# The decoded samples' state update, moved forward beside the branch projections, in a one-core hybrid decoder step

## The chip, the cores and the metric

The kernel runs on one core of one Trainium2 chip. The metric is the device time of one execution in microseconds. A core has TensorE (PE in the profile), VectorE (DVE), ScalarE (ACT), GpSimd (POOL) and SyncE (SP). Each works off its own queue in order; transfers are issued from the queues of SyncE, GpSimd and, seldom, ScalarE, and run on 16 DMA engines.

## The reference

One layer of a decoder trunk for 1024 prompt tokens and 8 decoded samples of one token each, 1024 channels wide, in float32. The part that matters here is the gated delta rule of the samples, with a state S of 128 x 128 for each of 8 samples (`b`) and 8 heads (`h`):

```python
def step(S, inp):
    q_t, k_t, v_t, b_t, g_t = inp
    S = S * jnp.exp(g_t)[..., None, None]
    delta = (v_t - jnp.einsum('bhk,bhkv->bhv', k_t, S)) * b_t[..., None]
    S = S + jnp.einsum('bhk,bhv->bhkv', k_t, delta)
    return S, jnp.einsum('bhk,bhkv->bhv', q_t, S)
...
y_a = _gdn_out(o_a, gdn_gate, lp['gdn_onorm_w']) @ lp['w_gdn_out']
...
y_b = o_b @ lp['w_swa_out']
mix = (jax.nn.sigmoid(ga) * y_a + jax.nn.sigmoid(gb) * y_b) @ lp['w_o']
```

The new states are an output, and the normed and gated result of the samples is the last eight columns of the input of `w_gdn_out`. `y_b` and `y_a` are the two branches.

## The kernel before

The 1032 tokens stand in the free dimension in three parts (`PARTS`): part 0 and part 1 of 384 tokens, part 2 of 264, the samples being its last 8. A projection (`project`) takes one block `j` of 128 output channels and one part `t`: 8 steps over the inner dimension with three matmuls each, because each operand is split into a high and a low half (`split`: ScalarE makes the high half at L129, VectorE the low one at L130). A weight block of 512 KB is loaded from SyncE's queue into a room `raw` (L135) and split into `wh` and `wl`. There is one room `raw` and two each of `wh` and `wl`.

`branches` does first the rest of the branch `w_swa_out` (14 projections: part 0 of six blocks, part 1 of all eight), and then the branch `w_gdn_out` with all three parts. Beside the 14 projections runs the generator `sample_delta`: before each projection one step of it is traced, up to its next `yield`. Its steps are: activation and squares of the samples' q, k, v; their norms (a matmul, `rows_rsqrt` with a power on GpSimd, `rows_spread` with a matmul); keys and queries `kq`; the products of k and q with the old states, 32 matmuls for each half of the heads (L1172); transposes (L1180); the deltas `dl`; their transpose and a store to a DRAM room `dlr` (L1194); the output's norm, which gives `osm`; and the new states.

For the new states of head `h` (L1210 to L1219), `dlr[h]` is read back, broadcast to all 128 partitions, into one of two rooms `d` in turn (L1214, SyncE). ScalarE multiplies it by the key, eight times, one for each sample (L1216); VectorE scales the old state and adds (L1217); GpSimd's queue stores the head's states (L1219). The rooms lie in `b1l`, the states in `b1h` and `b1l`, and the weights and parts of the next branch are loaded while this goes on.

The order on each engine is fixed when the kernel is built, by a planner that simulates the engines: an instruction goes to its queue when it is planned to be ready, and among those ready the one traced first. `issue_after(ins)` adds one rule: what is traced inside comes behind `ins` on the engine of `ins`. Here it puts the step's matmuls behind the last matmul of the projection before, and the step's transfers on SyncE behind the last weight load. It binds nothing on ScalarE, VectorE or GpSimd.

Of the kernel before, what the change touches and what calls it, by code (L numbers as in the profile page):

```python
# [12 lines left out]
AF = mybir.ActivationFunctionType  # L13
ALU = mybir.AluOpType
# [4 lines left out]
P = 128  # L19
NP = 1024  # L20
NS = 8
NT = NP + NS
KC = 8
H = 8
# [5 lines left out]
EARLY = (3, 4)  # L30
# [10 lines left out]
def bc(ap, dim, n):  # L41

    a = ap.unsqueeze(dim)
    shape = list(a.shape)
    shape[dim] = n
    return a.broadcast_to(shape)


def carver(*rooms):

    used = [0] * len(rooms)

    def small(*shape, r=0):
        n = 1
        for x in shape:
            n *= x
        v = rooms[r][:, used[r]:used[r] + n]
        used[r] += n
        letters = "abcd"[:len(shape)]
        return v.rearrange(f"p ({' '.join(letters)}) -> p {' '.join(letters)}", **dict(zip(letters, shape)))  # L60

    return small


class Step:
# [1055 lines left out]
    def sample_delta(self, pool2):  # L1121

        nc, I = self.nc, self.I
        zl, cw = self.zl, self.cw
        S0, load = self.S0, self.load_state
        small = carver(*(self.flat_room(pool2, "b2", x, 2) for x in "hl"))
        act, tmp = small(24, NS), small(24, NS)
        nc.vector.tensor_tensor(act, zl[:, 3:11, :].rearrange("p b c -> p c b"), bc(cw[:, 3, :], 2, NS), op=ALU.mult)
        nc.vector.tensor_tensor(act, act, self.gsp, op=ALU.add)
        nc.scalar.activation(tmp, act, AF.Tanh, scale=0.5)  # L1130
        nc.vector.scalar_tensor_tensor(act, tmp, 1.0, act, op0=ALU.add, op1=ALU.mult)

        flat = lambda a: a.rearrange("p a h b -> p (a h b)")
        f3 = lambda a: a.rearrange("p h b -> p (h b)")
        qk = act[:, 0:16, :].rearrange("p (a h) b -> p a h b", a=2)
        v = act[:, 16:24, :]
        sq = small(2, H, NS)
        nc.vector.tensor_tensor(sq, qk, qk, op=ALU.mult)
        wide = small(H, NS, 2 * NS)
        nc.gpsimd.memset(wide, 0.0)  # L1140
        yield
        c, db = (self.flat_room(self.b1, "b1", x, 2) for x in "hl")
        load(6, c)
        load(7, c)
        ps = self.t(self.psm, [P, 1], "mm")
        nc.tensor.matmul(ps, flat(sq), self.ones[:, 0:1], start=True, stop=True)
        r = self.rows_rsqrt(small, ps, P, 1.0, 4 * EPS)
        yield
        rl = self.rows_spread(*r).rearrange("p (a h b) -> p a h b", a=2, h=H)
        kq = self.const([P, H, NS, 2], "kq")  # L1150
        nc.vector.tensor_tensor(kq[:, :, :, 0], qk[:, 1], rl[:, 1], op=ALU.mult)
        nc.vector.scalar_tensor_tensor(kq[:, :, :, 1], qk[:, 0], P ** -0.5, rl[:, 0], op0=ALU.mult, op1=ALU.mult)
        for i in range(2):
            nc.vector.tensor_copy(wide.rearrange("p h b c -> p h (b c)")[:, :, i::2 * NS + 2], kq[:, :, :, i])
        yield
        pr = small(H, NS)
        nc.vector.tensor_tensor(pr, kq[:, :, :, 0], kq[:, :, :, 1], op=ALU.mult)
        dots = self.t(self.psm, [P, H, NS], "mm")
        nc.tensor.matmul(f3(dots), self.ones, f3(pr), start=True, stop=True)
        qkd = small(H, NS)  # L1160
        nc.vector.tensor_copy(qkd, dots)
        yield
        eg = self.egb[:, :, 0, :].rearrange("p b h -> p h b")
        beta = self.egb[:, :, 1, :].rearrange("p b h -> p h b")

        rows = small(2, P, r=1)
        nc.gpsimd.memset(rows, 0.0)
        for i in range(2):
            ps = self.t(self.psm, [P, P], "mm")
            for b in range(NS):  # L1170
                for h in range(4):
                    nc.tensor.matmul(ps[32 * h:32 * h + 2 * NS], wide[:, 4 * i + h, b, :], S0[4 * i + h][:, b, :],  # L1172
                                     start=b == 0, stop=b == NS - 1)
            for h in range(4):
                at = slice(32 * h, 32 * h + 2 * NS)
                (nc.scalar.copy if h % 2 else nc.vector.tensor_copy)(rows[at, i, :], ps[at])
            yield
        pks = self.t(self.psm, [P, 2 * P], "mm")
        for i in range(2):
            self.transpose(pks[:, i * P:(i + 1) * P], rows[:, i, :])  # L1180
        pks = pks.rearrange("p (h c) -> p h c", c=32)[:, :, :2 * NS].rearrange("p h (b a) -> p h b a", a=2)
        yield
        pk, dl, o = small(H, NS, 2), small(H, NS), small(H, NS)
        nc.vector.tensor_tensor(pk, pks, bc(eg, 3, 2), op=ALU.mult)
        nc.vector.tensor_scalar_mul(dl, v, 0.5)
        nc.vector.tensor_tensor(dl, dl, pk[:, :, :, 0], op=ALU.subtract)
        nc.vector.tensor_tensor(dl, dl, beta, op=ALU.mult)
        yield
        ps = self.t(self.psm, [H * NS, P], "mm")
        self.transpose(ps, f3(dl))  # L1190
        dlT = small(P, r=1)[:H * NS]
        nc.vector.tensor_copy(dlT, ps)
        dlr = self.t(self.dr, [H, NS, P], "dlr")
        nc.sync.dma_start(dlr.rearrange("h b v -> (h b) v"), dlT)  # L1194
        yield
        nc.vector.tensor_tensor(o, qkd, dl, op=ALU.mult)
        nc.vector.tensor_tensor(o, o, pk[:, :, :, 1], op=ALU.add)

        nc.vector.tensor_tensor(pr, o, o, op=ALU.mult)
        yield  # L1200
        ps = self.t(self.psm, [H * NS, 1], "mm")
        nc.tensor.matmul(ps, f3(pr), self.ones[:, 0:1], start=True, stop=True)
        r = self.rows_rsqrt(small, ps, H * NS, 1.0 / P, EPS)
        yield
        rl = self.rows_spread(*r).rearrange("p (h b) -> p h b", h=H)
        nc.vector.tensor_tensor(o, o, rl, op=ALU.mult)
        self.osm = self.const([P, H, NS], "osm")
        nc.vector.scalar_tensor_tensor(self.osm, o, self.onw, self.sgs, op0=ALU.mult, op1=ALU.mult)

        for h in range(H):  # L1210
            if h % 4 == 0:
                yield
            d = db[:, h % 2 * NP:h % 2 * NP + NP].rearrange("p (b v) -> p b v", b=NS)
            nc.sync.dma_start(d, dlr[h].unsqueeze(0).broadcast_to([P, NS, P]))  # L1214
            for b in range(NS):
                nc.scalar.activation(d[:, b, :], d[:, b, :], AF.Copy, scale=kq[:, h, b, 0:1])  # L1216
                nc.vector.scalar_tensor_tensor(S0[h][:, b, :], S0[h][:, b, :], self.egb[:, b, 0, h:h + 1], d[:, b, :],  # L1217
                                               op0=ALU.mult, op1=ALU.add)
            nc.gpsimd.dma_start(self.O[3][0][:, h].rearrange("b k v -> k b v"), S0[h])  # L1219

    def rows_rsqrt(self, small, ps, n, scale, eps):

# [109 lines left out]
    def branches(self, pool, pool2):  # L1332
        nc, I = self.nc, self.I
# [3 lines left out]
        samples, rows = self.sample_delta(pool2), self.last_rows()  # L1337
# [15 lines left out]
        weights = lambda j: self.load_w(I["w_swa_out"][0][:, j * P:(j + 1) * P])  # L1353
        ws = {j: weights(j) for j in (0, 1)}
        late = [(j, 0) for j in range(8) if j not in EARLY]
        for j, t in (*late[:2], *((j, t) for j in range(7) for t in (0, 1) if t or (j, t) in late[2:]), (7, 1), *late[-1:] * (7 not in EARLY)):
            with self.tc.issue_after(self.last_mm), self.tc.issue_after(self.w_load.ins):
                next(samples, None)
                if j > 3:
                    next(rows, None)  # L1360
            self.project(ws[j], ob, yb_out, (t,))
            if t and j < 6:
                ws[j + 2] = weights(j + 2)
            if t and j in (3, 4):
                with self.tc.issue_after(self.w_load.ins):
                    if j == 3:
                        oa = {0: self.load_part(pool2, self.oa, 0, rooms=first)}
                    else:
                        nc.sync.dma_start(ub[2], self.ubd[2].rearrange("j p n -> p j n"))
                        for j1 in EARLY:  # L1370
                            nc.sync.dma_start(ub[0][:, j1, :], self.ubd[0][j1])
# [700 lines left out]
```

## Time and profile before

| | |
|---|---|
| three runs | 2075.94, 2079.22 and 2079.28 us; median 2079.22 |
| the profiled execution | 2079.57 us, with a span of 2077.9 us from first to last instruction |
| mean granted clock of TensorE | 0.991 |
| DMA | 275.75 MB, mean 133 GB/s; 212.93 MB read from HBM |
| the branch `w_swa_out` beside the samples | about 1122 to 1188 us of the span |
| scalings of the states (L1216) | 1178.4 to 1218.3 us |
| stores of the states (L1219) | 1182.1 to 1220.5 us |

Times in rows are microseconds from the start of the span. A row of the timeline has start, duration, engine, line, operation, output and inputs, a count, and in brackets the idle time before it and what ended that. A row of the waits has who waited, for whom, the total, the number of waits and the longest. In rows by stretch the busy time and the number of instructions of each engine come first, then the granted clock, the DMA engines' busy share and GB/s.

### The profile page before, as it was taken

What the parts mean: (1) busy time and instruction counts of PE and PEld (TensorE: products, weight loads), DVE (VectorE), ACT (ScalarE), POOL (GpSimd) and SP (SyncE); (2) the same over time, 40 slices, a digit from 0 to 9 for tenths busy, and PEclk for the clock granted to TensorE, in tenths of its full rate; (3) what the DMA queues carried; (4) which work ended last, traced back from release to release, by engine and by line L of the source; (5) the groups of instructions that cost most, each with busy time, mean ns of one, the idle gap of its engine ahead of it and who ended that gap; (6) DMA issues with size and microseconds to landing.
All of it is one profiled execution on the core that took longest, in us unless ns stands there. A gap on an engine that the chain in (4) does not pass through costs nothing.

```text
span 2077.9 us, 41299 instructions
## 1 busy us (share of the span) xinstructions
PE 2011.2 (97%) x16245; PEld 1908.0 (92%) x16245; DVE 1353.8 (65%) x2714; ACT 900.6 (43%) x2233; POOL 521.6 (25%) x594
## 2 busy tenths in 40 slices
PE   7999999999999999989989999999999999999997
PEld 4987877799999999989989999999999999999997
DVE  4755767483655746656554575578886776778866
ACT  4664545443334343442442442345544544544443
POOL 2000000121321211211111000105566556443552
PEclk9999999999999999999999999999999999999999
DMA  8256443332322322312276874423233233487773
GB/s 292 72 145 206 138 168 116 94 99 66 82 82 57 77 70 52 91 41 57 67 200 186 257 225 133 144 65 97 88 106 113 88 97 92 135 294 271 268 261 114
DMA packets 301887, 275.75 MB, mean 133 GB/s; under 512 B 59730, under 2 KB 248111, under 8 KB 301676
## 3 DMA queue, kind: packets, MB, share of 16 engines
q1 hardware_dynamic: 295642, 252.14, 39.6%
q0 software_dynamic: 5552, 20.37, 2.8%
q8 instruction: 127, 2.08, 0.4%
q10 hardware_dynamic: 498, 0.61, 0.1%
q14 instruction: 68, 0.56, 0.1%
HBM read 212.93 MB, written 62.51 MB: 133 GB/s over the span
## 4 chain that ended last, share of the span: by engine, by line
PE 79%; DMA 8%; DVE 6%; ACT 3%; issue 2%; POOL 1%; SPq 1%; DVEq 0%; POOLq 0%; ACTq 0%
PE mm L180 18%; PE mm L181 18%; PE mm L182 18%; PE wv L180 2%; PE wv L182 2%; PE wv L181 2%; DMA ws<-in_w_ffn_down_dram 2%; PE pv L652 1%; PE wy L180 1%; PE wy L181 1%; PE wy L182 1%; DMA raw<-in_w_swa_out_dram 1%; PE pt L190 1%; PE tp L190 1%; PE mm L264 1%
## 5 line engine op out<-in xcount | busy, mean ns | idle before, releaser
L180 PE MATMUL mm<-b1h,wh 128*128 128x384 f32 (+1 forms) x1520 | 496.9, 328 | 4.2 <-ACT gt L1294 1.6
L181 PE MATMUL mm<-b1l,wh 128*128 128x384 f32 (+1 forms) x1520 | 489.4, 323 | 0.0
L182 PE MATMUL mm<-b1h,wl 128*128 128x384 f32 (+1 forms) x1520 | 487.7, 323 | 0.3 <-DVE wl L130 0.3
L180 PEld LDWEIGHTS mm<-b1h,wh 128*128 128x128 f32 x1520 | 286.5, 189 | 13.1 <-issue 4.6
L181 PEld LDWEIGHTS mm<-b1l,wh 128*128 128x128 f32 x1520 | 286.7, 189 | 5.1 <-issue 3.1
L182 PEld LDWEIGHTS mm<-b1h,wl 128*128 128x128 f32 x1520 | 286.0, 189 | 3.9 <-issue 2.8
L129 ACT ACTIVATE wh<-raw 128x1024 fp32r<-128x1024 f32 x83 | 87.0, 1049 | 124.3 <-PE mm L181 72.9
L130 DVE TENSOR_TENSOR wl<-raw,wh 128x1024 fp32r<-128x1024 f32 x82 | 101.3, 1236 | 59.9 <-ACT wh L129 57.4
L181 PE MATMUL mm<-pk,w 128*128 128x260 f32 (+1 forms) x440 | 124.6, 283 | 1.1 <-DVE pk L130 1.1
L180 PE MATMUL mm<-pk,w 128*128 128x260 f32 (+1 forms) x440 | 124.5, 283 | 0.0
L182 PE MATMUL mm<-pk,w 128*128 128x260 f32 (+1 forms) x440 | 124.4, 283 | 0.0
L130 DVE TENSOR_TENSOR w<-ws,w 128x512 fp32r<-128x512 f32 x88 | 77.8, 885 | 36.4 <-ACT w L129 36.2
L1626 ACT COPY bml<-mm 128x256 f32<-128x256 f32 (+1 forms) x132 | 48.9, 371 | 100.7 <-PE mm L182 98.9
L180 PE MATMUL mm<-bmh,w 128*128 128x260 f32 (+1 forms) x320 | 90.3, 282 | 0.0
L182 PE MATMUL mm<-bmh,w 128*128 128x260 f32 (+1 forms) x320 | 90.1, 282 | 0.0
L1681 DVE SCALAR_TENSOR_TENSOR fa<-fz,fcw,fa 128x512 f32<-128x512 f32 x88 | 75.5, 876 | 18.0 <-ACT fa L1679 17.7
L180 PE MATMUL mm<-b2h,wh 128*128 128x384 f32 (+1 forms) x256 | 83.1, 327 | 4.0 <-ACT wh L129 4.0
L181 PEld LDWEIGHTS mm<-pk,w 128*128 128x128 f32 x440 | 83.0, 189 | 1.3 <-DVE pk L130 1.3
L181 PE MATMUL mm<-b2l,wh 128*128 128x384 f32 (+1 forms) x256 | 83.6, 327 | 0.0
L180 PEld LDWEIGHTS mm<-pk,w 128*128 128x128 f32 x440 | 83.0, 189 | 0.2 <-ACT bml L1626 0.2
L182 PEld LDWEIGHTS mm<-pk,w 128*128 128x128 f32 x440 | 83.2, 189 | 0.0
L182 PE MATMUL mm<-b2h,wl 128*128 128x384 f32 (+1 forms) x256 | 82.9, 326 | 0.0
(645 smaller groups left out, 5888.9 us busy)
## 6 DMA issues: line engine op xcount, KB each, us to landing
raw<-in_w_in_dram SPq DMA_DIRECT2D x59, 512.0 KB
ws<-in_w_ffn_down_dram SPq DMA_DIRECT2D x55, 256.0 KB
raw<-xd SPq DMA_DIRECT2D x47, 258.0 KB
raw<-in_w_ffn_down_dram SPq DMA_DIRECT2D x47, 256.0 KB
raw<-in_w_ffn_gate_dram SPq DMA_DIRECT2D x22, 512.0 KB
raw<-in_w_ffn_up_dram SPq DMA_DIRECT2D x22, 512.0 KB
qst<-in_w_mod_dram SPq DMA_DIRECT2D x16, 512.0 KB
raw<-in_w_mod_dram SPq DMA_DIRECT2D x16, 512.0 KB
```

Source lines behind the costliest of these rows:

```text
L129: self.nc.scalar.activation(hi, x, AF.Copy)
L130: (eng or self.nc.vector).tensor_tensor(lo, x, hi.bitcast(F32), op=ALU.subtract)
L180: mm(ps, whi, xhi, start=first, stop=False, **kw)
L181: mm(ps, whi, xlo, start=False, stop=False, **kw)
L182: self.last_mm = mm(ps, wlo, xhi, start=False, stop=last, **kw).ins
L190: self.nc.tensor.transpose(out, in_, self.ident[:p, :p])
L264: nc.tensor.matmul(ps[32 * j:32 * j + 32], self.cT[:, k0 + j, :], ws[j // 2][:, j % 2, :], start=k0 == 0, stop=k0 > 0)
L652: nc.tensor.matmul(pv[64 * r:64 * r + 64], V[:, n - back, ch], ps[:, r::2, :], start=back == 0, stop=back == (n > 0))
L1626: self.last_copy = nc.scalar.copy(r[p, i], x[p])
L1681: nc.vector.scalar_tensor_tensor(ai[:, c:e], zi[:, j + c:j + e], col(j), ai[:, c:e], op0=ALU.mult, op1=ALU.add)
```

## The change

Three things change. The two halves of the product with the old states are one step instead of two. Before each of the first four projections two steps of the generator are traced, later one. The new states are updated in four groups of two heads, traced right behind the store of the deltas and between the steps of the output's norm, instead of in two groups of four heads behind it; and the broadcasts of `dlr` go from SyncE's queue to GpSimd's, where the stores of the states are already. With 12 steps in place of 14, the deltas are traced before the fourth projection instead of the eighth and ninth, and the last two heads before the eighth projection instead of the fourteenth.

```diff
@@ -1174,7 +1174,7 @@
             for h in range(4):
                 at = slice(32 * h, 32 * h + 2 * NS)
                 (nc.scalar.copy if h % 2 else nc.vector.tensor_copy)(rows[at, i, :], ps[at])
-            yield
+        yield
         pks = self.t(self.psm, [P, 2 * P], "mm")
...
@@ -1193,30 +1193,35 @@
         dlr = self.t(self.dr, [H, NS, P], "dlr")
         nc.sync.dma_start(dlr.rearrange("h b v -> (h b) v"), dlT)
         yield
+        def states(*heads):
+            for h in heads:
+                d = db[:, h % 2 * NP:h % 2 * NP + NP].rearrange("p (b v) -> p b v", b=NS)
+                nc.gpsimd.dma_start(d, dlr[h].unsqueeze(0).broadcast_to([P, NS, P]))
+                for b in range(NS):
+                    nc.scalar.activation(d[:, b, :], d[:, b, :], AF.Copy, scale=kq[:, h, b, 0:1])
+                    nc.vector.scalar_tensor_tensor(S0[h][:, b, :], S0[h][:, b, :], self.egb[:, b, 0, h:h + 1], d[:, b, :],
+                                                   op0=ALU.mult, op1=ALU.add)
+                nc.gpsimd.dma_start(self.O[3][0][:, h].rearrange("b k v -> k b v"), S0[h])
+
         nc.vector.tensor_tensor(o, qkd, dl, op=ALU.mult)
         nc.vector.tensor_tensor(o, o, pk[:, :, :, 1], op=ALU.add)
 
         nc.vector.tensor_tensor(pr, o, o, op=ALU.mult)
+        states(0, 1)
         yield
         ps = self.t(self.psm, [H * NS, 1], "mm")
         nc.tensor.matmul(ps, f3(pr), self.ones[:, 0:1], start=True, stop=True)
         r = self.rows_rsqrt(small, ps, H * NS, 1.0 / P, EPS)
+        states(2, 3)
         yield
         rl = self.rows_spread(*r).rearrange("p (h b) -> p h b", h=H)
         nc.vector.tensor_tensor(o, o, rl, op=ALU.mult)
         self.osm = self.const([P, H, NS], "osm")
         nc.vector.scalar_tensor_tensor(self.osm, o, self.onw, self.sgs, op0=ALU.mult, op1=ALU.mult)
 
-        for h in range(H):
-            if h % 4 == 0:
-                yield
-            d = db[:, h % 2 * NP:h % 2 * NP + NP].rearrange("p (b v) -> p b v", b=NS)
-            nc.sync.dma_start(d, dlr[h].unsqueeze(0).broadcast_to([P, NS, P]))
-            for b in range(NS):
-                nc.scalar.activation(d[:, b, :], d[:, b, :], AF.Copy, scale=kq[:, h, b, 0:1])
-                nc.vector.scalar_tensor_tensor(S0[h][:, b, :], S0[h][:, b, :], self.egb[:, b, 0, h:h + 1], d[:, b, :],
-                                               op0=ALU.mult, op1=ALU.add)
-            nc.gpsimd.dma_start(self.O[3][0][:, h].rearrange("b k v -> k b v"), S0[h])
+        states(4, 5)
+        yield
+        states(6, 7)
...
@@ -1353,9 +1358,11 @@
-        for j, t in (*late[:2], *((j, t) for j in range(7) for t in (0, 1) if t or (j, t) in late[2:]), (7, 1), *late[-1:] * (7 not in EARLY)):
+        order = (*late[:2], *((j, t) for j in range(7) for t in (0, 1) if t or (j, t) in late[2:]), (7, 1), *late[-1:] * (7 not in EARLY))
+        for i, (j, t) in enumerate(order):
             with self.tc.issue_after(self.last_mm), self.tc.issue_after(self.w_load.ins):
-                next(samples, None)
+                for _ in range(2 if i < 4 else 1):
+                    next(samples, None)
                 if j > 3:
                     next(rows, None)
             self.project(ws[j], ob, yb_out, (t,))
```

## The prediction

> **What bounds the kernel now.** I read the page first, then the waits of TensorE, the busy time by stretch around the changed code, the chain of waits there, and the queues of SyncE, ScalarE and GpSimd.
>
> ```profile
> span 2077.9 us, 41299 instructions
> PE 2011.2 (97%) x16245; PEld 1908.0 (92%) x16245; DVE 1353.8 (65%) x2714; ACT 900.6 (43%) x2233; POOL 521.6 (25%) x594
> PE mm L180 <- ACT wh L129: 4.4, 2, 4.0
> core 0: us, PE busy (x) PEld busy (x) DVE busy (x) ACT busy (x) POOL busy (x), PEclk, DMA share, GB/s
> 1142.00:1157.00 15.00, 15.00 (x174) 14.26 (x163) 6.05 (x13) 3.15 (x6) 0.00 (x0) 1.00 0.42 122
> 1157.00:1172.00 15.00, 15.00 (x89) 14.63 (x88) 8.93 (x15) 6.04 (x8) 0.00 (x0) 1.00 0.97 305
> 1172.00:1192.80 20.80, 20.80 (x119) 20.20 (x117) 13.88 (x39) 11.84 (x31) 2.71 (x4) 1.00 0.92 310
> 1192.80:1196.80 4.00, 0.04 (x1) 0.00 (x0) 2.65 (x9) 3.40 (x10) 0.60 (x2) 1.00 1.10 378
> 1196.80:1201.00 4.20, 4.16 (x20) 4.16 (x21) 4.18 (x6) 3.15 (x4) 0.86 (x1) 0.59 1.06 410
> 1201.00:1281.00 80.00, 80.00 (x509) 80.00 (x508) 50.33 (x126) 28.13 (x82) 5.74 (x8) 1.00 0.51 153
> ```
>
> TensorE has matmuls in flight for 97% of the span, and the change removes none of them. It can only win idle time or clock. In the stretch that it touches, there is one hole: 4.00 us from 1192.8, and behind it 4.20 us at a granted clock of 0.59, which lose (1 - 0.59) x 4.20 = 1.7 us. Together 5.7 us (0.27%) can be won; from 1201 to 1281 TensorE is full. The chain says what made the hole:
>
> ```profile
> 1168.91 5.59 DMA dlr<-b2l
> 1174.52 3.85 DMA b1l<-dlr
> 1178.39 4.80 ACT b1l L1216 x16
> ...
> 1184.60 8.71 DMA b1l<-dlr
> ...
> 1193.40 0.41 ACT b1l L1216
> ...
> 1195.84 0.95 ACT wh L129
> 1196.80 0.04 issue
> 1196.84 0.44 PE mm L180
> ```
>
> The matmuls wait for a split of a weight (L129). ScalarE's queue holds that split behind eight scalings of a sample's state (L1216), and these wait for a broadcast that took 8.71 us. So the sample work, late as it is, stands ahead of the second weight of the next projection.
>
> **The change part by part.** First, what the weights allow. There is one room for a raw weight: the next load is issued when the split of the last has ended.
>
> ```profile
> 1156.69 0.38 SPq L135 DMA_DIRECT2D raw<-in_w_swa_out_dram  x1
> 1162.70 0.39 SPq L135 DMA_DIRECT2D raw<-in_w_swa_out_dram  x1
> 1171.66 0.38 SPq L135 DMA_DIRECT2D raw<-in_w_swa_out_dram  x1
> 1178.98 0.38 SPq L135 DMA_DIRECT2D raw<-in_w_gdn_out_dram  x1
> 1187.08 0.38 SPq L135 DMA_DIRECT2D raw<-in_w_gdn_out_dram  x1
> 1198.08 0.38 SPq L135 DMA_DIRECT2D raw<-in_w_gdn_out_dram  x1
> ```
>
> Five cycles, 6.0, 9.0, 7.3, 8.1 and 11.0 us, 41.4 in all; the shortest stands for a load that meets little. Over 5 x 6.0 = 30.0 the second lost 3.0 and the third 1.3, before any state was updated; the fourth 2.1 and the fifth 5.0, beside the first four heads. TensorE kept up until the fifth, so each microsecond that this chain loses or wins against 41.4 is one more or less of the 4.0.
>
> *First steps two at a time.* No instruction is added. Where each step's matmuls stood, and the evacuation that closes the third projection:
>
> ```profile
> 1140.15 0.56 DVE L1341 TENSOR_TENSOR t<-mm,gt 128x384 f32<-128x384 f32 x1 [2.05 <-PE mm L182]
> 1141.08 0.30 PE L1172 MATMUL mm<-b1h,b2h 128*16 128x128 f32 x3
> 1147.66 0.29 PE L1172 MATMUL mm<-b1l,b2h 128*16 128x128 f32 x2
> 1162.32 0.27 PE L190 MATMUL mm<-ident,b2h 128*64 128x128 f32 x1
> ```
>
> The transpose of the deltas stood behind the eighth projection (1162.3) and now stands behind the third (1140.2): 22.1 us earlier, so the first state block moves from 1178.4 to about 1156.3. The matmuls and small vector steps are the same work in another order, and the projections around them cover the hops between engines. Where a step comes so soon that this cover is gone, TensorE waits for another engine's operation; the nearest row is the end of the hole, 0.95 + 0.04 us from split to matmul. A gain is out, since TensorE was full there (15.00 of 15.00 us). I take nothing, because seven steps still find a projection each, and keep two such hops, 2 us, for the upper end. The first projections are not late for it: their weights were loaded before.
>
> *States two heads per step.* The same 64 scalings and 64 updates:
>
> ```profile
> L1216 ACT ACTIVATE b1l<-b1l,kq 128x128 f32<-128x128 f32 x64 | 19.5, 389 | 5.8 <-DMA b1l<-dlr 5.8
> L1217 DVE SCALAR_TENSOR_TENSOR b1h<-b1h,egb,b1l 128x128 f32<-128x128 f32 x40 | 11.4, 342 | 0.4 <-ACT b1l L1216 0.4
> L1217 DVE SCALAR_TENSOR_TENSOR b1l<-b1l,egb,b1l 128x128 f32<-128x128 f32 x24 | 6.8, 344 | 1.6 <-ACT b1l L1216 1.6
> 1193.40 2.45 ACT L1216 ACTIVATE b1l<-b1l,kq 128x128 f32<-128x128 f32 x8 [1.58 <-DMA b1l<-dlr]
> 1208.10 2.18 DVE L1217 SCALAR_TENSOR_TENSOR b1l<-b1l,egb,b1l 128x128 f32<-128x128 f32 x8
> ```
>
> Four heads took from 1178.39 to the end of the block of 1193.40 (1195.85), 17.5 us, set by two rooms for broadcasts. Eight then take 35, from 1156.3 to 1191.3: across all five weight cycles, and over just before the fifth's split. On ScalarE state blocks then fill 19.5 / 35 = 0.56 of the time, on VectorE 18.2 / 35 = 0.52. A split that comes at a random moment waits half a block: 0.56 x 1.23 + 0.52 x 1.09 = 1.26 us per weight, 6.3 for five. In the new chain this replaces the 2.1 and 5.0 of the last two: 30.0 + 3.0 + 1.3 + 6.3 = 40.6, against 41.4. The 4.0 become 3.2, in pieces. The ends: no meeting at all, chain 34.3, no wait; a whole block on ScalarE before each weight, 5 x 2.45 = 12.3, chain 46.6, wait 9.2. I take 3.2, since the blocks fill about half. In pieces of one to two microseconds TensorE's clock should stay: the rows show it fall only behind 4.00 us of nothing. Behind the waiting ScalarE block stand the split, VectorE's second half of it, and then the matmuls.
>
> *Broadcasts on GpSimd's queue.* SyncE loses eight issues, GpSimd gets them.
>
> ```profile
> L1214 SPq DMA_DIRECT2D b1l<-dlr x8: 320/349/668, 1174.5 to 1210.3; - x8
> b1l<-dlr SPq DMA_DIRECT2D x8, 512.0 KB
> SPq L1214 <- DMA dlr<-b2l: 2.5, 1, 2.5
> L1219 POOL DMA_DIRECT2D out_dram<-b1h x5: 885/885/959, 1182.1 to 1220.5; - x5
> DMA to landing us min/median/max: 4.8/6.8/8.3
> 1172.24 0.55 POOL L125 TENSOR_TENSOR b2l<-b2l,mhalf 64x1 f32<-64x1 f32 x1 [36.82 <-DVE b2l L1225]
> 1183.10 0.24 ACT L129 ACTIVATE b2h<-osm 128x64 fp32r<-128x64 f32 x1
> ```
>
> On SyncE this frees 8 x 0.35 us and the wait of 2.5 us; no weight was issued late for it (each issue follows its split), so nothing. On GpSimd eight issues of 0.885 us are 7.1 us on an engine that had 2.71 us of work in 20.80: hidden. New is the order: broadcast h + 2 waits until VectorE has left head h, and the stores and the one power of the samples' norm (0.55 us) queue behind it. That delays the power by one pair's 17.5 / 2 = 9 us at most. It stands five projections earlier than its 1172.2, and what comes of it is first split at 1183.1, so this is hidden; without those five projections the samples' part of the next projection would wait the 9 us. No row shows a broadcast from GpSimd; its nearest are the stores, 4.8 to 8.3 us, against 3.85 and 8.71 on SyncE. So between a gain and a loss of 4 us for each broadcast, hidden by two rooms until the last pair; I take no change, as the stores' median of 6.8 is near the mean of the two broadcasts, 6.3.
>
> The Trainium skill has a rule against this move: "SBUF — State Buffer", section "SBUF: two separate sides", holds that GpSimd cannot write its descriptors while VectorE runs in a two-port mode, and tells of a transfer of 620 ns that took 3100. By that, an estimate from the page, a pair is 2.5 us slower, the last one passes 1200, its broadcast wait and block (1.58 + 2.45) stand before the fifth weight again, and the sum would be 2081.1. The trace speaks against it: 885 ns was least and median, 959 the most, with VectorE busy for 13.88 of 20.80 us.
>
> **The sum.** -4.0 (hole) - 1.7 (clock) + 3.2 (shorter waits) = -2.5 us on the profiled execution's 2079.57: 2077.1. The median of the three runs is 2079.22, so I stand 0.1% under it. Runs spread 3.3 us; 0.2%, 4.2 us, is about what tells a change from none: 2075.1 to 2083.4.
>
> **The rivals.** *The weights get free.* If the blocks fall between the splits, or the chain starts before 1156, nothing of the 4.0 stays: 2073.9. For it: DMA share 0.42 and ScalarE 3.15 of 15 us before 1157, room for the first pairs. Against: the first pair hardly gets there before 1156.
>
> *Nothing moves.* The last pair still meets the fifth weight, now at about 1190, and the transfer of the weight is as slow, since the same engines carry the broadcasts: the hole stays, 2079.6. For it: a last block that ends at 1191.3 stands within 2 us of the point where TensorE ran dry. The Trainium skill, "DMA: Bandwidth & Descriptors", section "Issuing engines are not separate DMA queues", says that another issuing engine saves its issue time alone; by that rule the move of the broadcasts is worth nothing here, and the trace of before, with all on SyncE, cannot contradict it.
>
> *Slower: the transfers starve the weights.* Broadcasts and the stores of the same heads are 16 x 0.52 = 8.4 MB. By 1192.8 about 3.5 MB of them had moved (four broadcasts and the stores of the three heads then done, not all landed); now all have, 4.9 MB more, at 310 to 378 GB/s 13 to 16 us. Spare is 0.58 x 5 us before 1157, 0.03 x 15 and 0.08 x 20.8 behind, 5.0 us. If the weights pay for all that is missing, the chain is 8 us longer, the waits 12.0 and the sum +6.3: 2085.9. It decides from 1.7 us of added chain, where it eats the clock's gain. For it: shares of 0.97 and 0.92. Against: 305 GB/s there, 410 later, so a share near one is not yet full.
>
> **How the numbers follow.** Forecast 0.34 (its own range 2074.5 to 2080), weights free 0.25, nothing 0.14, starved 0.25 (a fifth of it within 0.2%), else 0.02. Faster: 0.25 and a quarter of the forecast, with a bit of the rest 0.35. Slower: 0.20 and a bit, 0.22. Same: 0.43. The range reaches from below the free case to the starved one's price: 2072 to 2086.
>
> **What would show it.** Right: first L1216 near 1156, last near 1190; no wait of 4 us on the split and no stretch of clock under 0.8 between 1190 and 1205; waits of 1 to 2 us on splits between 1160 and 1195. Wrong: weight loads from 1156 that take over 9 us each (starved), the hole with L1216 ahead of it (nothing moves), or waits of TensorE on the sample steps between 1130 and 1145, which I priced at nothing.

## The result and the profile after

The changed kernel takes 2095.14 us (median of six runs, 2090.96 to 2097.28), the kernel before 2079.68 us beside it: 1.0069 times as long, 95% interval 1.0055 to 1.0084. It is slower by 0.7%, where I had forecast 2077.1 us and a range up to 2086. The profiled execution took 2097.28 us, the slowest of the six. From the page of the changed kernel, and from its waits of TensorE between 1120 and 1240 us (total, number of waits, longest):

```profile
span 2095.5 us, 41301 instructions
PE 2018.0 (96%) x16245; PEld 1912.4 (91%) x16245; DVE 1358.8 (65%) x2714; ACT 900.6 (43%) x2233; POOL 525.5 (25%) x602
```

```profile
PE mm L180 <- ACT wh L129: 8.9, 2, 6.9
PE mm L181 <- DVE b2l L130: 1.3, 3, 0.6
PE mm L180 <- ACT b2h L129: 1.3, 1, 1.3
```

The one wait of 4.0 us for a weight's split has become two of 8.9 us together, and the input's splits are now waited for too. The busy time by stretch shows where (TensorE is the first pair after the stretch's length; granted clock, DMA share and GB/s are the last three):

```profile
core 0: us, PE busy (x) PEld busy (x) DVE busy (x) ACT busy (x) POOL busy (x), PEclk, DMA share, GB/s
1142.00:1157.00 15.00, 15.00 (x195) 14.23 (x194) 7.60 (x18) 3.97 (x7) 0.00 (x0) 1.00 0.39 111
1157.00:1172.00 15.00, 15.00 (x88) 14.35 (x87) 10.40 (x23) 7.90 (x17) 1.70 (x4) 1.00 0.93 313
1172.00:1180.80 8.80, 8.80 (x52) 8.80 (x52) 4.78 (x12) 3.61 (x10) 2.87 (x4) 1.00 1.06 375
1180.80:1188.80 8.00, 1.15 (x7) 0.83 (x5) 2.81 (x5) 2.92 (x5) 0.00 (x0) 0.71 0.83 280
1188.80:1193.00 4.20, 4.12 (x13) 4.00 (x14) 4.14 (x13) 4.20 (x16) 0.52 (x1) 0.50 0.52 161
1193.00:1205.00 12.00, 11.24 (x61) 10.92 (x59) 5.70 (x16) 4.39 (x12) 3.82 (x6) 0.94 0.92 281
1205.00:1217.00 12.00, 8.57 (x45) 7.67 (x46) 9.63 (x21) 8.74 (x21) 1.44 (x2) 0.91 0.77 250
1217.00:1225.00 8.00, 8.00 (x53) 8.00 (x53) 3.86 (x10) 3.40 (x9) 0.91 (x1) 0.92 0.68 212
1225.00:1291.00 66.00, 66.00 (x413) 66.00 (x412) 38.49 (x90) 16.96 (x47) 2.56 (x4) 1.00 0.41 117
```

From 1142 on TensorE is idle 6.85 + 0.08 + 0.76 + 3.43 = 11.1 us, and the lower clock costs 1.15 x 0.29 + 4.12 x 0.50 + 11.24 x 0.06 + 8.57 x 0.09 + 8 x 0.08 = 4.5 us; before it was 4.0 + 1.7. That is 9.9 us more. The stage's last evacuation moved from 1284.8 to 1297.2, 12.4 us, of which 1.0 was there when the stage began; so 9.9 of 11.4 us are in these rows. The span is 17.6 us longer: the other 5.2 come behind the stage, where the planned order differs too: from the stage's end to the end of the span TensorE idles 20.9 us where it idled 17.5, and 20 us of it (1337.2 to 1357.2) show a clock of 0.91 where the same stretch before (1324.8 to 1344.8) shows 1.00, which costs 1.8 us.

Why a weight was late stands on SyncE's queue (part loads of the next branch are now L1255, the store of the deltas L1194):

```profile
1157.82 0.38 SPq L135 DMA_DIRECT2D raw<-in_w_swa_out_dram  x1
...
1158.88 0.51 SPq L1194 DMA_DIRECT2D dlr<-b2l  x1
...
1164.20 0.37 SPq L135 DMA_DIRECT2D raw<-in_w_swa_out_dram  x1
...
1169.84 0.40 SPq L1255 DMA_DIRECT2D b2l<-oa  x1
...
1174.42 2.04 SPq L1255 DMA_DIRECT2D b2l<-oa  x3
...
1177.10 0.38 SPq L135 DMA_DIRECT2D raw<-in_w_swa_out_dram  x1
...
1190.11 0.38 SPq L135 DMA_DIRECT2D raw<-in_w_gdn_out_dram  x1
1196.06 3.61 SPq L1255 DMA_DIRECT2D b2l<-oa  x4
...
1200.37 0.38 SPq L135 DMA_DIRECT2D raw<-in_w_gdn_out_dram  x1
...
1214.65 0.38 SPq L135 DMA_DIRECT2D raw<-in_w_gdn_out_dram  x1
```

The five cycles of the one `raw` room are now 6.4, 12.9, 13.0, 10.3 and 14.3 us: 56.8, against 41.4. Before, part 2 of the input (1 MB) and part 1 (1.5 MB) were issued at 1179.5 and 1187.6, each just behind a weight (1178.98 and 1187.08):

```profile
1179.47 1.03 SPq L1250 DMA_DIRECT2D b2l<-oa  x2
...
1187.56 4.23 SPq L1250 DMA_DIRECT2D b2l<-oa  x4
```

Now part 2 stands ahead of the eighth weight and part 1 ahead of the second weight of `w_gdn_out`. ScalarE, VectorE and TensorE show what the eighth weight paid:

```profile
1167.73 0.26 ACT L129 ACTIVATE b2h<-osm 128x64 fp32r<-128x64 f32 x1 [0.30 <-DVE osm L1220]
1168.48 2.45 ACT L1201 ACTIVATE b1l<-b1l,kq 128x128 f32<-128x128 f32 x8 [0.49 <-DMA b1l<-dlr]
...
1187.77 1.06 ACT L129 ACTIVATE wh<-raw 128x1024 fp32r<-128x1024 f32 x1 [1.49 <-DMA raw<-in_w_swa_out_dram]
...
1212.31 1.06 ACT L129 ACTIVATE wh<-raw 128x1024 fp32r<-128x1024 f32 x1 [1.60 <-DMA raw<-in_w_gdn_out_dram]
...
1222.31 2.44 ACT L1201 ACTIVATE b1l<-b1l,kq 128x128 f32<-128x128 f32 x8
```

```profile
1172.66 1.23 DVE L130 TENSOR_TENSOR wl<-raw,wh 128x1024 fp32r<-128x1024 f32 x1 [1.00 <-ACT wh L129]
```

```profile
1188.88 0.69 PE L180 MATMUL mm<-b2h,wh 128*128 128x384 f32 x1 [6.93 <-ACT wh L129]
```

The room was free at 1173.89, the load went out at 1177.10 (3.2 us behind the part), and its split began at 1187.77, 10.7 us after the issue. This time it is the transfer that ScalarE waits for, not a state block ahead of the split: ScalarE was idle before. The second `w_gdn_out` weight took 1200.37 to 1212.31, 11.9 us.

### The profile page after: what moved, and what is told of

Its sections match the earlier page's. It is cut to its first block, busy times and chain, and to the rows that moved or that the text cites. A ratio compares the mean times of both kernels' runs of the same rounds, so it can differ in the third digit from the quotient of the medians.

```text
span 2095.5 us, 41301 instructions
## 1 busy us (share of the span) xinstructions
PE 2018.0 (96%) x16245; PEld 1912.4 (91%) x16245; DVE 1358.8 (65%) x2714; ACT 900.6 (43%) x2233; POOL 525.5 (25%) x602
## 4 chain that ended last, share of the span: by engine, by line
PE 77%; DVE 8%; DMA 7%; issue 3%; ACT 3%; SPq 1%; POOL 1%; DVEq 0%; POOLq 0%; ACTq 0%
PE mm L180 17%; PE mm L181 17%; PE mm L182 17%; PE wv L180 2%; PE wv L182 2%; PE wv L181 2%; PE pv L652 1%; PE wy L182 1%; PE wy L180 1%; PE wy L181 1%; PE pt L190 1%; DVE x L1479 1%; PE tp L190 1%; PE mm L264 1%; PE sc L614 1%
```

## Experiments

The theory: the pairs of first steps end the samples' chain earlier; the state traffic (8 broadcasts and 8 stores of 0.5 MB) then falls on the weights of 1170 to 1200, and in the planned order on SyncE the part loads pass the weights. Rivals: GpSimd's queue, the grouping of the states, the order alone, the traffic alone.

**The order put back.** After the changed kernel, the first weights of `w_gdn_out` are traced ahead of the parts:

```diff
-        oa[2] = self.load_part(pool2, self.oa, 2, last=self.osm)
-        oa[1] = self.load_part(pool2, self.oa, 1)
+        gdn = lambda j: self.load_w(I["w_gdn_out"][0][:, j * P:(j + 1) * P])
+        g0 = gdn(0)
+        with self.tc.issue_after(self.w_load.ins):
+            oa[2] = self.load_part(pool2, self.oa, 2, last=self.osm)
+        g1 = gdn(1)
+        with self.tc.issue_after(self.w_load.ins):
+            oa[1] = self.load_part(pool2, self.oa, 1)
...
```

> The changed kernel with one thing put back: on SyncE's queue the loads of the parts for the second branch stand behind the weights again, as before the change (eighth w_swa_out weight, first w_gdn_out weight, part 2, second w_gdn_out weight, part 1). States, steps and broadcasts as changed. Theory 1, queue order: the two holes of the changed kernel (6.9 us in front of the eighth weight, about 4 us in front of the second w_gdn_out weight) come from the 1 MB and 1.5 MB loads that stand ahead of those weights; here both holes go, and the time is 2076 to 2082, within 0.2% of before or faster. Theory 2, saturation: the state traffic, moved to where the weights are loaded, starves them whatever the order; the time stays above 2088 and the loads of these weights still take over 9 us.

2086.15 us, 1.0039 (1.0024 to 1.0054). So 9.0 of the 15.5 us go with the order; the chain of weights falls from 56.8 to 45.6 us. The rest stays: the eighth weight, issued at 1174.2 with no part ahead of it, was split only at 1182.3, and TensorE still waits:

```profile
PE mm L180 <- ACT wh L129: 6.7, 2, 4.9
```

**Part 2 alone.** Only part 2 is held behind the eighth weight.

```diff
-        oa[2] = self.load_part(pool2, self.oa, 2, last=self.osm)
+        with self.tc.issue_after(self.w_load.ins):
+            oa[2] = self.load_part(pool2, self.oa, 2, last=self.osm)
```

> The changed kernel with part 2 of the input held behind the eighth weight on SyncE; part 1 stays ahead of the second gdn weight. The order of both was worth 9 us. Theory (a part costs by its bytes: 1.0 and 1.5 MB): 2091 to 2092, eighth weight in 8 to 9 us, second gdn weight over 11. Rival (the eighth weight decides, since all behind it is late with it): 2086. Rival (part 1 decides): 2095.

2087.07 us, 1.0038 (1.0024 to 1.0053): as the whole order, within the noise. Its weight chain, from 1154.8 to 1204.6, is 49.8 us. So the bytes of a part, by which I had expected 2091 to 2092, do not set the price; the place of one load, the eighth weight, does most of it. The ten runs spread from 2080.37 to 2091.68, and the profile is of one of 2082.83. TensorE's waits in it, and SyncE's queue there:

```profile
PE mm L180 <- ACT wh L129: 4.6, 2, 2.9
```

```profile
1171.78 0.38 SPq L135 DMA_DIRECT2D raw<-in_w_swa_out_dram  x1
1172.78 2.21 SPq L1255 DMA_DIRECT2D b2l<-oa  x3
...
1182.05 0.37 SPq L135 DMA_DIRECT2D raw<-in_w_gdn_out_dram  x1
```

**Small transfers.** The changed kernel, in its own order, with one of a head's eight samples broadcast and one stored:

```diff
-                nc.gpsimd.dma_start(d, dlr[h].unsqueeze(0).broadcast_to([P, NS, P]))
-                for b in range(NS):
-                    nc.scalar.activation(d[:, b, :], d[:, b, :], AF.Copy, scale=kq[:, h, b, 0:1])
+                nc.gpsimd.dma_start(d[:, 0:1, :], dlr[h][0:1].unsqueeze(0).broadcast_to([P, 1, P]))
+                for b in reversed(range(NS)):
+                    nc.scalar.activation(d[:, b, :], d[:, 0, :], AF.Copy, scale=kq[:, h, b, 0:1])
...
-                nc.gpsimd.dma_start(self.O[3][0][:, h].rearrange("b k v -> k b v"), S0[h])
+                nc.gpsimd.dma_start(self.O[3][0][0:1, h].rearrange("b k v -> k b v"), S0[h][:, 0:1])
```

> The changed kernel, its order on SyncE's queue unchanged (parts ahead of weights), with the states' transfers cut to an eighth: each head's broadcast brings the delta of one sample, which all eight scalings use, and each store writes the state of one sample. It leaves out seven eighths of the deltas and of the stored states; the number of instructions on every engine is the same. Theory 1, queue order: only the order matters, so the holes stay and the time is 2088 to 2096. Theory 2, saturation: without 7.3 MB beside the weights they land in time; 2078 to 2084. If both count, in equal shares as the first four runs suggest, 2084 to 2090.

2077.34 us, 0.9998 (0.9985 to 1.0011). With an eighth of the traffic, the whole loss is gone, though the parts still stand ahead of the weights. Its profiled execution (2080.91) still shows a wait, about as long as the 4.0 us of before:

```profile
PE mm L180 <- ACT wh L129: 4.7, 2, 3.9
```

The two causes therefore do not add: the order costs its 9 us only while the state traffic is there (with small transfers, the next run, putting it back wins only 0.2 us).

**Small transfers, weights first.** Both edits.

> The kernel with the weights ahead of the parts on SyncE's queue, with the same cut of the states' transfers to an eighth (one sample's delta and one sample's stored state for each head). Both theories together: order and state traffic are all that the change cost, so 2072 to 2079, at or under the kernel before, and no wait of TensorE on a weight's split over 2 us. If 2084 or more is left, something else that the early steps do costs it: the scalings ahead of the splits on ScalarE's queue, or the steps' own waits.

2077.14 us, 0.9992 (0.9979 to 1.0006). The chain is 39.7 us and the wait is nearly gone:

```profile
PE mm L180 <- ACT wh L129: 0.6, 1, 0.6
```

So even with its transfers made small and the weights put first, the change cannot be told from the kernel before. The hole and its clock, 5.7 us, were a small prize.

**Which of the transfers.** The cut for the stores alone, and for the broadcasts alone.

> The changed kernel with one sample's new state stored for each head instead of eight (1/8 of the bytes); the broadcasts whole. Theory (all the state traffic competes with weights and parts, byte by byte): half of the gain that the cut of both gave, some 2086, weight chain about 53 us. Rival A (the broadcasts do it, because ScalarE's scalings and the split behind them wait for them): as the changed kernel, 2095, chain 57. Rival B (the stores do it): 2077, chain 49.

> The changed kernel with one sample's delta broadcast for each head (1/8 of the bytes; all eight scalings take it); the stores whole. Theory: 2086, chain about 53 us, as with the stores cut. Rival A: 2077, chain 49. Rival B: 2095, chain 57.

Stores cut: 2090.09 us, 1.0053 (1.0039 to 1.0067), chain 53.2 us. Broadcasts cut: 2087.82 us, 1.0043 (1.003 to 1.0057), chain 52.3 us. The two intervals overlap, and that of the stores also overlaps with the changed kernel's (1.0055 to 1.0084). Neither kind does it alone: either cut leaves a clear loss, and only both together end it. With the stores cut the planner also moves ScalarE's work: a state block that waits 4.05 us for its broadcast (1201.88) now stands ahead of the split of the second `w_gdn_out` weight (1207.16), so this run does not isolate the stores. In the second no broadcast of 0.5 MB is left that could be late in front of ScalarE's splits, yet the weights are almost as late.

**Broadcasts on SyncE, and on GpSimd alone.** First the changed kernel with `nc.sync.dma_start` for the broadcasts, then the kernel before with `nc.gpsimd.dma_start` for them and nothing else.

> The changed kernel with the broadcasts back on SyncE's queue. On that queue the parts still stand ahead of the weights. Theory 1, queue order: still slow, 2088 to 2100, since two broadcasts more stand ahead of the eighth weight. Theory 3, GpSimd's queue: the broadcasts on their own ring take DMA time from the weights, and on SyncE's they cannot; then the time falls back to within 0.3% of before, under 2086.

> The kernel before with the broadcasts on GpSimd's queue and nothing else changed; the order of weights and parts on SyncE's queue is that of before. Theory 1, queue order: within 0.3% of before, 2074 to 2085; if anything faster, since the second w_gdn_out weight no longer stands behind a broadcast. Theory 3, GpSimd's queue: slower by 5 us or more.

2095.24 us, 1.0083 (1.0065 to 1.0101), and 2080.06 us, 1.0011 (0.9995 to 1.0028). The queue of the broadcasts makes no difference that can be measured, either way. The Trainium skill, "DMA: Bandwidth & Descriptors", section "Issuing engines are not separate DMA queues", says that another issuing engine saves only the time of the issue; both runs agree.

**Pairs alone.** The kernel before, with the first steps two at a time (one product step, the loop over two steps for the first four projections), the states in two groups of four heads behind the norm, broadcasts on SyncE.

> The kernel before with the first steps two at a time and nothing else: states in two groups of four heads, broadcasts on SyncE. Theory (the earlier end of the samples' chain does it, whatever the grouping and the queue): as the changed kernel, 2092 to 2097, parts of the input ahead of the eighth weight on SyncE, weight chain over 52 us. Rival (four groups of two, strewn between the weights, do it): at most 2084, chain under 47.

2092.8 us, 1.0068 (1.0054 to 1.0082): the whole loss. The parts pass the weights here too, and the chain is 59.1 us:

```profile
1162.82 0.38 SPq L135 DMA_DIRECT2D raw<-in_w_swa_out_dram  x1
...
1174.56 1.98 SPq L1250 DMA_DIRECT2D b2l<-oa  x3
1180.50 0.38 SPq L135 DMA_DIRECT2D raw<-in_w_swa_out_dram  x1
1191.50 0.38 SPq L135 DMA_DIRECT2D raw<-in_w_gdn_out_dram  x1
...
1202.15 0.67 SPq L135 DMA_DIRECT2D raw<-in_w_gdn_out_dram  x1
...
1215.57 0.38 SPq L135 DMA_DIRECT2D raw<-in_w_gdn_out_dram  x1
```

```profile
PE mm L180 <- ACT wh L129: 9.7, 3, 8.0
```

**One step at a time.** The changed kernel with `for _ in range(1):`, so the other two parts of the change without the pairs.

> The changed kernel with one step before each projection, states two heads per step and broadcasts on GpSimd's queue. On SyncE's queue the eighth weight stands ahead of part 2 again, but part 1 still ahead of the second w_gdn_out weight. Theory 1, queue order: one of the two holes is left, the second; 2081 to 2090, between before and the changed kernel. Theory 2, saturation: it goes by when the states start; here they start about 15 us later than in the changed kernel, and the time is within 0.2% of before.

2078.68 us, 1.0004 (0.9993 to 1.0014). The states begin at 1173.1 instead of 1168.5, only 4.6 us later, where I had expected some 15. The eighth weight goes out at 1169.7, ahead of part 2; part 1 still stands ahead of the second `w_gdn_out` weight, and that alone brings no loss here. TensorE's waits are short (the profile is of the fastest execution, 2075.06):

```profile
PE mm L180 <- ACT wh L129: 2.6, 3, 1.7
```

**The order alone, on the kernel before.** The second `w_gdn_out` weight is held behind part 1 (`issue_after` on the last part load), states late as before.

> The kernel before with one thing changed: on SyncE's queue the 1.5 MB of part 1 stand ahead of the second w_gdn_out weight instead of behind it. States, steps and broadcasts as before. Theory 1, queue order: that weight lands 3 to 5 us later, and the hole of 4.0 us in front of it grows to 7 to 9 us: 2083 to 2089. Theory 2, saturation: the order of the two makes no difference in a queue that is full anyway: within 0.1% of before.

2081.78 us, 1.0018 (1.0007 to 1.0028): some 3 us, below the 2083 to 2089 of theory 1 and above the 0.1% of theory 2. The second `w_gdn_out` weight took 11.4 us to its split (1187.71 to 1199.15), but TensorE's longest wait is one of 3.2 us, for a split of the input, no longer than the 4.0 of before; where the 3 us arise I have not found. The eighth weight keeps its place here, so this tests part 1 and not part 2.

**One step at a time, weights first.** Both edits of the kernels above.

> One step before each projection, states two heads per step, broadcasts on GpSimd's queue, and the weights ahead of the parts on SyncE's queue: a candidate for better than both. Theory 1, queue order: the kernel with one step at a time had the second w_gdn_out weight behind part 1 and waits of 2.6 us on splits; with the order put back it wins 2 to 4 us: 2073 to 2077. Theory 2, saturation: same as with one step at a time, within 0.1% of before.

2091.16 us, 1.0062 (1.004 to 1.0083): worse than without the order, which I had not foreseen. The five cycles are only 46.2 us, but the sixth is 21.0 (17.1 in the kernel before): on ScalarE the split of the next weight stands behind a state block whose broadcast is late, the old hole one weight further on.

```profile
1217.94 2.44 ACT L1201 ACTIVATE b1l<-b1l,kq 128x128 f32<-128x128 f32 x8 [6.33 <-DMA b1l<-dlr]
1220.29 1.04 ACT L129 ACTIVATE wh<-raw 128x1024 fp32r<-128x1024 f32 x1
```

So "weights first" is no rule by itself: put in by hand, it also moves what the planner places on the other engines. Why this order helps with pairs and hurts without was not taken further. No version that does the whole work beat the kernel before.

## Why the prediction was wrong

*"First steps two at a time. I take nothing."* This is the step that failed. The pairs alone take 1.0068 times as long, as much as the whole change. I priced the steps' instructions and hops, and TensorE was indeed full from 1142 to 1180.8, as I said. What I left out is that the order on SyncE is planned anew when the samples' chain ends elsewhere: the split of `osm`, which the samples' part of the input needs, moved from 1183.1 to 1167.7, and part 2's load from behind a weight to ahead of it. That place costs time together with the states' transfers: with these cut to an eighth, the same order costs nothing (2077.34 us). I had named every queue that an instruction was moved past, but not the loads that nobody moved. That the planner did this because part 2 was planned to be ready sooner is my reading of how it works; the runs show only the order and its price.

*"22.1 us earlier, so the first state block moves from 1178.4 to about 1156.3."* It moved to 1168.5, 9.9 us. The transpose of the deltas moved by 4.2 us only:

```profile
1158.17 0.27 PE L190 MATMUL mm<-ident,b2h 128*64 128x128 f32 x1
```

I had taken the place in the trace order for the time. But the steps wait for each other's small operations: the product with the old states still ran at 1142.9 and 1146.8, against 1141.1 and 1147.7. The other 5.7 us came between transpose and first scaling: the store of the deltas was issued 0.7 us after the transpose, where it had been 6.6.

*"Eight heads take 35 us."* They took 56.3, from 1168.5 to 1224.8. The row that I used, 17.5 us for four, came from a stretch with one broadcast of 3.85 and one of 8.71 us; now the median is 7.4 us from issue to landing, and the two rooms chain them:

```profile
b1l<-dlr POOLq DMA_DIRECT2D x8, 512.0 KB, 7.4
```

*"1.26 us per weight, 6.3 for five"*, blocks on ScalarE and VectorE in front of the splits. The wrong price: of the 15.4 us that the chain grew, 9.0 are in two loads (10.7 us from issue to split where it was 5.0, and 11.9 where it was 8.7), with ScalarE idle just before both splits, and 5.6 are weights that waited on SyncE behind a part, though their room was free (3.2 and 2.4 us). With small transfers all 64 scalings and updates are still there, though the planner moves some to the other side of a split, and no loss is left.

*"each microsecond that this chain loses or wins against 41.4 is one more or less of the 4.0."* This rate was wrong too. With small transfers the chain is 49.4 us, 8.0 longer, yet TensorE waits 4.7 us for these splits instead of 4.0; in the changed kernel it is 15.4 longer, and TensorE idles 7.1 us more. The five cycles were also too few: over six, the kernel before has 58.4 us (1156.69 to 1215.13) and the changed one 65.9 (1157.82 to 1223.69); the eight kernels over 2086 us have 60.7 or more, and the six under 2082 have 60.2 or less. That sorts these runs and is no law.

*"In pieces of one to two microseconds TensorE's clock should stay."* It did not: the pieces were 6.9 and 2.0 us, and the clock fell to 0.50 behind both (below), which cost 4.5 us instead of none.

*"Broadcasts on GpSimd: nothing."* Right: 1.0011 on the kernel before, no measurable difference on the changed one. The rule of the Trainium skill, "SBUF — State Buffer", section "SBUF: two separate sides", that GpSimd is held up in writing its descriptors while VectorE runs in a two-port mode, found no support: VectorE was busy for 10.40 of the 15 us in which the first two were issued, yet the eight issues took 0.54 to 0.56 us each. No trace here shows in which mode VectorE ran, so this is no strict test of it.

```profile
1163.48 1.11 POOL L1199 DMA_DIRECT2D b1l<-dlr  x2 [2.80 <-DMA dlr<-b2l]
```

*"Slower: the transfers starve the weights"*, which I gave 0.25 and 2085.9 us. Its sign was "weight loads from 1156 that take over 9 us each", and two did. The mechanism was half of the right one, and so was the size: 8 us of longer chain (the lower end of the 8 to 11 that my figures give), measured 15.4. The order put back brings the time to 2086.15, near the price that I gave the traffic by itself, but that is luck: the chain there is 45.6 us, 4.2 longer than 41.4 and not 8. My way to the price was wrong as well. I added up bytes over the whole stretch. In the 44 us from 1157 to 1201 the engines moved no more than before (rows above: about 13 MB, against 14). The traffic hurts by when it comes: 375 GB/s at a share of 1.06 from 1172 to 1180.8, just when the eighth weight was due, and then 161 to 281 GB/s, while with one `raw` room no further weight could be loaded until that one was split.

## What to carry to other kernels

When a side chain is moved forward, price not only its own instructions but the transfers that its earlier end lets go, and look for what they now stand ahead of on each issue queue. Where weights come through one room, a single late load holds up those that follow; so look at what stands ahead of that load and what moves beside it in the very microseconds in which it is due, not at the bytes of the stage. And size the prize first: here all that could be won was 5.7 us, and with the transfers made small it could not be told from nothing.

## What the runs showed of the hardware

The shortest cycles of the one room, load and split of 512 KB, were about 6 us (5.9 to 6.4); the eighth weight's load took 10.7 us in the changed kernel, with 280 to 375 GB/s moving (5.0 us in the kernel before). What moves does not set this time by itself: with small transfers, part 2 still ahead of it, the same load took 8.2 us (1175.20 to 1183.36) at 219 GB/s. I had taken the 410 GB/s of another stretch as a sign that room was left at a share near one; this load was slow all the same.

TensorE's clock went with the length of the hole only in part. With holes of at most 2.9 us (the run with part 2 alone held) every stretch from 1142 to 1225 shows 1.00; with one of 3.9 us (small transfers) the 12 us around it show 0.86, and behind the one of 6.9 us the changed kernel shows 0.50 over 4.2 us. But the changed kernel also shows 0.50 from 1215 to 1218, behind a hole of only 2.0 us (1211.5 to 1213.4) with shorter ones before it: from 1205 to 1215 TensorE was busy for 6.57 us. By stretch, the run with part 2 held, whose hole of 2.9 us ends at 1203.4, and then the one with small transfers:

```profile
1193.00:1205.00 12.00, 9.08 (x55) 8.76 (x55) 7.76 (x18) 7.65 (x19) 1.44 (x2) 1.00 0.85 281
1205.00:1217.00 12.00, 12.00 (x83) 12.00 (x82) 8.99 (x26) 6.50 (x20) 2.36 (x3) 1.00 0.79 244
```

```profile
1181.00:1193.00 12.00, 8.53 (x40) 8.41 (x41) 7.59 (x20) 6.79 (x18) 1.63 (x4) 0.86 0.40 117
```

The Trainium skill, "TensorE: Matmul & The Clock Gate", section "Part 1: The HAM clock gate (the "warmup" mystery)", puts the fall behind at least one idle window of about 3.4 us; the holes of 2.9, 3.9 and 6.9 us agree, the one of 2.0 us does not.
